# Where one layer's modulation steps are traced, how many go with a tile of the swiglus, and which queue loads them

## The chip, the cores and the metric

The kernel runs on one core of a Trainium2 chip. The time is device microseconds (us) of one execution; three executions of the kernel before gave 2858.24, 2849.52 and 2848.32 us, with a median of 2849.52 us. A fourth execution was profiled: it took 2853.62 us, and its span from the first instruction to the last is 2851.7 us.

## The reference

Two blocks run one after the other on a sequence of 512 tokens of width 1024, in float32. The first block has two layers: gated linear attention (GLA) and a swiglu, then latent attention (MLA) and a swiglu. The second block mixes a pooling and a convolution branch, and then gathers experts. Ahead of all this, each layer turns the conditioning vector `c` into six modulation vectors, and each of its two halves uses three of them:

```
c_act = silu(c)
for i in range(DEPTH):
    mod = c_act @ ada_w[i] + ada_b[i]
    sh1, sc1, g1, sh2, sc2, g2 = split(mod, 6)
    h = rmsnorm(x, norm_mix[i]) * (1 + sc1) + sh1
    x = x + g1 * mixer(h)
    h = rmsnorm(x, norm_ffn[i]) * (1 + sc2) + sh2
    x = x + g2 * swiglu(h)
```

`ada_w[i]` is 1024 x 6144, so a layer's modulation reads 24 MB; the second block has one such layer more.

## The kernel before, in words

Activations lie transposed: eight tiles `x[k]` of 128 channels x 512 tokens. Each projection is a sum of three matmuls, since the weights and the activations are split into a high and a low part (`whi`/`wlo`, `hh`/`hl`, `fh`/`fl`; line 241, ScalarE copies the high part and VectorE subtracts). Weights come as units of 1 MB (`raw<-wst`, line 268) from SyncE's queue, 16 blocks of 128 x 128 in each; two tiles of a swiglu's input projection, which make one tile of its hidden width, use one unit.

The modulation isn't computed on TensorE. `ada` (lines 315 to 325) is a Python generator. One step of it loads 128 rows of the transposed `ada_w` (512 KB, `araw`, of which there are two buffers, `ARAW`), issued by SyncE's queue (line 320), and multiplies and sums them against silu(c) on VectorE in one instruction (`dot`, line 313), called a dot below. Eight steps make one of the six vectors. A layer's `mods` columns 16:24 are its first gate, 24:32 and 32:40 the shift and the scale of its second norm, 40:48 its second gate.

`step(n)` (line 329) traces n further steps at the place in the code where it stands, and `rest()` all that are left. There are three such streams around the change:

- In the GLA, 24 steps of layer 0 (columns 16 to 40). The order of the GLA's parts is `GLA_ORDER` (line 58): q are projections of queries and keys, i the work inside chunks (`intra`: eight levels, at each of which GpSimd subtracts, ScalarE takes the exponential, VectorE multiplies twice in lines 637 and 638, TensorE multiplies in line 644 and VectorE copies under a mask in line 650), v values, r the output gate's projections, o the outputs. Three steps follow each q (line 708), two each r (line 717), and `rest()` stands ahead of the output projection (line 724). `gains` (line 339) makes the second norm's factor from the scale, before `output_norm` begins (line 727).
- In the first swiglu (`ffn(0)`), 56 steps: the last vector of layer 0 and all of layer 1 (line 760). `step(FST)`, with `FST` = 3, follows each of the 22 tiles of the hidden width (line 749), eleven in each half.
- In the second swiglu (`ffn(1)`), 48 steps of the second block's layer (line 945), with the same calls.

In each half of a swiglu eleven tiles are made (per tile: 48 matmuls, then silu on ScalarE, a product on VectorE in line 742, and the split into `fh` and `fl`), and then the output projection runs over them (lines 750 and 751). `output_norm` (line 451) runs the output projection of an attention in six full tiles, then the last two in halves together with the norm (`tail`, `modulated`).

The place in the code isn't the place in an engine's queue. The framework plans ahead with costs of its own and fixes each engine's order at build time: an instruction goes to its engine when its plan has it ready and the engine free; of several that are ready the one traced first goes first (weights are let ahead by `high_priority`). So a step may be planned far ahead of the place where it is traced, when its engine is free in the plan. On the chip the engines then run their instructions in that order, each waiting for its own inputs.

Of the kernel before, what the change touches and what calls it, by code (L numbers as in the profile page):

```python
# [21 lines left out]
P = 128  # L22
S = 512
D = 1024
KD = 8
# [29 lines left out]
FIRST = 3  # L55
M0 = 6
HNU = 4
GLA_ORDER = "q0 q1 i0 q2 i1 q3 i2 v0 r0 r1 i3 r2 r3 o0 o1 v1 r4 r5 r6 r7 o2 o3"
RECT = 64
KXL = 1  # L60
ST = (3, 2, 2)
ARAW = 2
APART = 4
FST = 3
SPILL = [NA // 2 + (2 * i + 1) * (P // 2 - NA // 2) // (2 * NSP) for i in range(NSP)]
LAST = 2
GSC = 2.0 ** 14
# [127 lines left out]
def block_kernel(ctx, tc, x_in, cs_in, wst, vec, cst, gmask, smask, pos, ada1, ada2, wgate, keys, ust, uex, vex, out):  # L195
    nc = tc.nc
    V, A_, T_, G_, SP = nc.vector, nc.scalar, nc.tensor, nc.gpsimd, nc.sync
# [10 lines left out]
    def bank(tag="mm"):  # L208
        return ps.tile([P, S], F32, tag=tag, bufs=4, name=tag)
# [14 lines left out]
    def vc(name, i, n=1):  # L224
        return vt[:, VOFF[name] + i:VOFF[name] + i + n]

    x = [keep.tile([P, S], F32, name=f"x{k}") for k in range(KD)]
    hh = [keep.tile([P, S], F32R, name=f"hh{k}") for k in range(KD)]
    hl = [keep.tile([P, S], F32R, name=f"hl{k}") for k in range(KD)]
    mods = [keep.tile([P, 48], F32, name=f"mod{l}") for l in range(3)]  # L230
# [27 lines left out]
    def blk(name, n=1, eng=None):  # L258
        while SEQ[state["i"]][0] == "pad":
            state["i"] += 1  # L260
        i = state["i"]
        assert SEQ[i][0] == name, (SEQ[i], name)
        u, o = divmod(i, UB)
        assert o + n <= UB
        if state.get("u") != u:
            with tc.high_priority(state["ahead"]):
                raw = wp.tile([P, UB * P], F32, tag="raw", bufs=RAW, name="raw")
                SP.dma_start(raw, wst[u])
                state["w"] = parts(raw, G_ if name in POOL_LO else eng)
            state["u"] = u  # L270
        state["i"] = i + n
        return part(state["w"], o * P, n * P)

    def mm3(out_, wh, wl, ah, al, first, last):
        T_.matmul(out_, wh, ah, start=first, stop=False)  # L275
        T_.matmul(out_, wh, al, start=False, stop=False)  # L276
        state["mm"] = T_.matmul(out_, wl, ah, start=False, stop=last)  # L277
# [15 lines left out]
    def proj(name, ah, al, tag="mm"):  # L293
        if state["pre"]:
            return state["pre"].pop(0)
        p = bank(tag)
        n = len(ah)
        for k in range(n):
            wh, wl = blk(name)
            mm3(p, wh, wl, ah[k], al[k], k == 0, k == n - 1)  # L300
        return p
# [9 lines left out]
    def dot(out_, w, sc, op=V.scalar_tensor_tensor):  # L311

        op(out=w, in0=w, scalar=1.0, in1=sc, op0=ALU.mult, op1=ALU.mult, accum_out=out_)  # L313

    def ada(l, w, sc, bias, pieces=range(6)):

        for p in pieces:
            for n in range(p * KD, (p + 1) * KD):
                raw = mn.tile([P, D], F32, tag="araw", bufs=ARAW, name="araw")
                SP.dma_start(raw, w[n * P:(n + 1) * P, :])  # L320
                dot(mods[l][:, n:n + 1], raw, sc)
                if n % KD == KD - 1:
                    m = mods[l][:, p * KD:(p + 1) * KD]
                    V.tensor_add(m, m, bias[:, p * KD:(p + 1) * KD])
                yield
# [3 lines left out]
    def step(n=1):  # L329
        for _ in range(n):  # L330
            next(side["g"], None)

    def rest():
        for _ in side["g"]:
            pass

    def gains(l, which, g):

        o = sca[:, (l * 2 + which) * KD:(l * 2 + which + 1) * KD]
        sc_ = mods[l][:, (1 + 3 * which) * KD:(2 + 3 * which) * KD]  # L340
        V.scalar_tensor_tensor(o, sc_, 1.0, g, op0=ALU.add, op1=ALU.mult)
        return o
# [90 lines left out]
    def tail(name, ah, al, gate, sqs, norm):  # L433

        ws = [[blk(name) for _ in ah] for _ in range(2)]
        for half in range(2):
            cs = halves(half)
            for i, w in enumerate(ws):
                n = KD - 2 + i
                p = bank()  # L440
                for k, (wh, wl) in enumerate(w):
                    mm3(p[:, cs], wh, wl, ah[k][:, cs], al[k][:, cs], k == 0, k == len(ah) - 1)
                residual(n, p, gate, cs)
                for sq, scale in sqs:
                    sq.add(x[n], scale=scale and scale(n), half=half)
            norm(half)

    def residual(n, p, gate, cs=slice(0, S)):
        V.scalar_tensor_tensor(x[n][:, cs], p[:, cs], gate[:, n:n + 1], x[n][:, cs], op0=ALU.mult, op1=ALU.add)

    def output_norm(name, ah, al, gate, gain, shift, first):

        sq = Sq(mn, "a", KD, D)
        for n in range(KD - 2):
            residual(n, proj(name, ah, al), gate)
            sq.add(x[n])
        tail(name, ah, al, gate, [(sq, None)],
             lambda half: modulated(bcast(sq.rsqrt("n", half)), gain, shift, half))
        ahead(first, hh, hl)
# [5 lines left out]
    with tc.tile_pool(name="st", bufs=1, reuse_waits="tile") as st, tc.high_priority(2 * AHEAD):  # L465
# [62 lines left out]
        w = weights()  # L528
# [9 lines left out]
        for k in range(KD):  # L538
# [11 lines left out]
            w = w_  # L550
# [4 lines left out]
    with tc.tile_pool(name="gla", bufs=1, reuse_waits="tile") as gp:  # L555
# [147 lines left out]
        bs, n = gates()  # L703
        for what in GLA_ORDER.split():
            kind, h = what[0], int(what[1])
            if kind == "q":
                qk[h] = [first.pop(0) if first else qk_tile(i) for i in range(2)]
                step(3)
            elif kind == "i":
                ins[h] = intra(bs[h], *qk[h])  # L710
            elif kind == "v":
                vn[h] = values()
            elif kind == "r":
                p = proj("gla_w_in", hh, hl)
                sr[h] = gp.tile([P, S], F32, tag="sr", bufs=4, name="sr")
                A_.activation(sr[h], p, AF.Silu)
                step(2)
            else:
                if h == 2:
                    for i, o in enumerate(og):  # L720
                        split(hh[i], hl[i], o)
                    og = []
                og += output(h, vn[h // 2], [sr[2 * h], sr[2 * h + 1]], *ins[h])
        rest()
        for i, o in enumerate(og):
            split(hh[4 + i], hl[4 + i], o)
        output_norm("gla_w_out", hh, hl, mods[0][:, 16:24], gains(0, 1, vc("norm_ffn", 0, KD)),
                    mods[0][:, 24:32], "ffn_w_in")


    def ffn(l, sqs, norm, first):
        gate = mods[l][:, 40:48]
        norm_ = state["norm"]
        with tc.tile_pool(name=f"ffn{l}", bufs=1, reuse_waits="tile") as fp:
            for half in range(2):
                fh, fl = [], []
                for i in range(11):
                    p = proj("ffn_w_in", hh, hl)
                    s = fp.tile([P, S], F32, tag="s", bufs=2, name="s")
                    A_.activation(s, p, AF.Silu)  # L740
                    p = proj("ffn_w_in", hh, hl)
                    V.tensor_mul(s, s, p)
                    a = fp.tile([P, S], F32R, name=f"fh{i}")
                    c = fp.tile([P, S], F32R, name=f"fl{i}")
                    split(a, c, s)
                    fh.append(a)
                    fl.append(c)
                    with tc.issue_after(norm_.ins):
                        step(FST)
                for n in range(KD - 2 * half):  # L750
                    residual(n, proj("ffn_w_out", fh, fl), gate)
                    if half:
                        for sq, scale in sqs:
                            sq.pool = sq.pool or fp
                            sq.add(x[n], scale=scale and scale(n))
            rest()
            tail("ffn_w_out", fh, fl, gate, sqs, norm)
            ahead(first, hh, hl)
# [52 lines left out]
    with tc.tile_pool(name="mla", bufs=1, reuse_waits="tile") as mp:  # L811
# [124 lines left out]
        for h in range(MLA_H):  # L936
# [2 lines left out]
            attend(h, prs.pop(h))  # L939
            if h + 2 < MLA_H:  # L940
                queries(h + 2)
        output_norm("mla_w_out", hh, hl, mods[1][:, 16:24], gains(1, 1, vc("norm_ffn", KD, KD)),
                    mods[1][:, 24:32], "ffn_w_in")

    side["g"] = ada(2, ada2, silu_c(1), vc("ada_b_2", 0, 48))


# [25 lines left out]
    with tc.tile_pool(name="b2", bufs=1, reuse_waits="tile") as bp:  # L973
# [45 lines left out]
        for g in range(4):  # L1019
            p = proj("w_in_2", hh, hl)  # L1020
            step(4)
            w = WINDOWS[g]
# [63 lines left out]
        for n in range(8):  # L1086
# [1 line left out]
            V.tensor_mul(sg[8 + n], sg[8 + n], p)  # L1088
            V.tensor_add(sg[n], sg[n], sg[8 + n])
            split(hh[n], hl[n], sg[n])  # L1090
        output_norm("w_out_2", hh, hl, mods[2][:, 16:24], gains(2, 1, vc("norm2_g_2", 0, KD)),
                    mods[2][:, 24:32], "w_query_2")

    main.close()
# [2 lines left out]
    with tc.tile_pool(name="peer", bufs=1, reuse_waits="tile") as pp:  # L1097
# [38 lines left out]
        with tc.tile_pool(name="sel", bufs=1, reuse_waits="tile") as sp:  # L1136
# [179 lines left out]
            for h in range(PH):  # L1316
                qq, ql = [], []
                for half in range(2):
# [3 lines left out]
                    l = sp.tile([P, P], F32, name=f"ql{h}_{half}")  # L1322
# [21 lines left out]
            for j2 in range(NA // 2):  # L1344
                up(j2, eng=V)
                if j2 == HNU:
                    mark = state["mm"]

        with tc.tile_pool(name="exp", bufs=1, reuse_waits="tile") as ep:
# [81 lines left out]
            for g in range(P // GJ):  # L1431
# [13 lines left out]
                for half in range(2):  # L1445
# [12 lines left out]
                    for dd in range(4):  # L1458
                        n = half * 4 + dd
# [95 lines left out]
```

## Time and profile before

| What | Value |
|---|---|
| median of three runs | 2849.52 us |
| the profiled execution | 2853.62 us, span 2851.7 us |
| TensorE busy | 95% of the span |
| VectorE busy | 75% |
| ScalarE, GpSimd busy | 37%, 29% |
| GLA after its first norm | about 66 to 282 us of the span |
| its output projection and norm | 282 to 336 us |
| first swiglu | 336 to about 720 us |
| second swiglu | 933 to about 1310 us |

Busy shares are averages over stages with different limits. What one engine's idle time costs is read from the stage: which wait ends last there.

### The profile page before, as it was taken

The page shows a single profiled execution, that of the slowest core. Times are in us where ns is not written, and L with a number is a line of the kernel's source. Part 1 is how long each engine was busy: PE and PEld are TensorE (multiplying, and loading weights), DVE is VectorE, ACT ScalarE, POOL GpSimd, SP SyncE. Part 2 cuts the span into 40 slices and gives each one's busy share as a digit, 9 for nine tenths or more (in the row PEclk, how much of TensorE's full clock was granted, in tenths as well). Part 3 has the DMA queues.
Part 4 walks back from the last instruction along what each step waited for, and adds up shares of the span by engine and source line. Part 5 has one row for each costly group of instructions (what it writes and reads, how often), then busy time and mean ns, then how long its engine had stood idle before and what let it go on. Part 6 is the DMA issues. An engine that isn't in the chain of part 4 may idle for free. (4 is left out here: it accounts for less than half of the span.)

```text
span 2851.7 us, 39033 instructions
## 1 busy us (share of the span) xinstructions
PE 2717.1 (95%) x14889; PEld 2447.4 (86%) x14889; DVE 2150.5 (75%) x3981; ACT 1064.6 (37%) x1530; POOL 816.3 (29%) x586
## 2 busy tenths in 40 slices
PE   6799999999999999999999999899999999999998
PEld 4677887888778878888778888889999999999998
DVE  8874766435776773348976798888899889988996
ACT  4443322222543322234443336654333343333332
POOL 4531100001011000001631423433545445545561
PEclk9899999999999999999999999999999999999999
DMA  6441477432212673222223236666999999999993
GB/s 265 140 136 60 145 260 258 140 104 78 74 45 74 229 257 129 94 89 90 74 89 103 77 110 192 204 191 229 362 350 342 356 339 346 336 341 329 345 342 136
DMA packets 184363, 560.62 MB, mean 197 GB/s; under 512 B 13248, under 2 KB 66912, under 8 KB 157680
## 3 DMA queue, kind: packets, MB, share of 16 engines
q1 hardware_dynamic: 142352, 407.08, 41.0%
q0 software_dynamic: 41472, 151.01, 14.2%
q8 instruction: 117, 1.92, 0.3%
q14 instruction: 70, 0.57, 0.1%
q10 hardware_dynamic: 352, 0.03, 0.0%
HBM read 527.32 MB, written 30.75 MB: 196 GB/s over the span
## 5 line engine op out<-in xcount | busy, mean ns | idle before, releaser
L241 ACT CAST whi<-raw 128x1024 fp32r<-128x1024 f32 x510 | 535.1, 1051 | 1197.4 <-PE mm L276 617.5
L277 PE MATMUL mm<-hh,wlo 128*128 128x512 f32 (+2 forms) x2544 | 899.4, 354 | 9.4 <-DVE wlo L241 9.4
L276 PE MATMUL mm<-hl,whi 128*128 128x512 f32 (+2 forms) x2544 | 900.6, 355 | 7.4 <-DVE hl L427 6.6
L275 PE MATMUL mm<-hh,whi 128*128 128x512 f32 (+2 forms) x2544 | 899.9, 355 | 2.0 <-ACT hh L426 1.4
L241 DVE TENSOR_TENSOR wlo<-raw,whi 128x1024 fp32r<-128x1024 f32 x472 | 585.7, 1242 | 264.8 <-ACT whi L241 251.5
L277 PEld LDWEIGHTS mm<-hh,wlo 128*128 128x128 f32 x2544 | 482.5, 190 | 59.3 <-DVE wlo L241 11.6
L276 PEld LDWEIGHTS mm<-hl,whi 128*128 128x128 f32 x2544 | 482.9, 190 | 56.0 <-DVE hl L427 7.9
L275 PEld LDWEIGHTS mm<-hh,whi 128*128 128x128 f32 x2544 | 482.6, 190 | 49.1 <-ACT hh L426 1.8
L241 POOL TENSOR_TENSOR wlo<-raw,whi 128x1024 fp32r<-128x1024 f32 x38 | 90.9, 2398 | 907.5 <-ACT whi L241 866.2
L1376 POOL DMA_INDIRECT rows<-vex,eidx x144 | 223.9, 1555 | 203.3 <-DVE y L1390 186.7
L1376 POOL DMA_INDIRECT rows<-uex,eidx x144 | 215.9, 1499 | 217.0 <-DVE rows L1380 162.6
L313 DVE SCALAR_TENSOR_TENSOR araw<-araw,sc 128x1024 f32<-128x1024 f32 x128 | 160.5, 1256 | 96.5 <-DMA araw<-ada 95.9
L1390 DVE SCALAR_TENSOR_TENSOR y<-rows,act,y 128x1024 f32<-128x1024 f32 x142 | 181.7, 1280 | 6.9 <-DMA rows<-vex,eidx 6.3
L1380 DVE SCALAR_TENSOR_TENSOR rows<-rows,hn 128x1024 f32<-128x1024 f32 x144 | 169.8, 1220 | 15.2 <-DMA rows<-uex,eidx 15.2
L275 PE MATMUL mm<-fh,whi 128*128 128x512 f32 (+1 forms) x396 | 148.0, 374 | 10.2 <-ACT fh L241 10.2
L276 PE MATMUL mm<-fl,whi 128*128 128x512 f32 (+1 forms) x396 | 148.3, 375 | 2.0 <-DVE fl L241 2.0
L277 PE MATMUL mm<-fh,wlo 128*128 128x512 f32 (+1 forms) x396 | 147.6, 373 | 0.0
L1306 PE MATMUL acc<-oa,ob 128*128 128x128 f16 x736 | 95.6, 297 | 18.6 <-POOL oa L1297 11.0
L1297 POOL TENSOR_TENSOR oa<-o,o 128x1024 f16<-128x1024 f16 x30 | 81.8, 2742 | 83.4 <-DVE o L1283 57.4
L1306 PEld LDWEIGHTS <-ob 128*128 128x128 f16 x736 | 81.5, 119 | 27.9 <-issue 18.9
L1309 ACT ACTIVATE stage<-acc 128x512 f32<-128x512 f32 x92 | 90.0, 1103 | 27.5 <-PE acc L1306 15.7
L275 PEld LDWEIGHTS mm<-fh,whi 128*128 128x128 f32 x396 | 77.1, 195 | 23.4 <-ACT fh L241 11.1
(1381 smaller groups left out, 4685.4 us busy)
## 6 DMA issues: line engine op xcount, KB each, us to landing
raw<-wst SPq DMA_DIRECT2D x127, 1024.0 KB, 4.9
araw<-ada SPq DMA_DIRECT2D x128, 512.0 KB, 4.5
raw<-ust SPq DMA_DIRECT2D x64, 1024.0 KB, 6.5
raw<-vex SPq DMA_DIRECT2D x64, 1024.0 KB, 7.8
gd<-stage SPq DMA_DIRECT2D x23, 1024.0 KB, 4.8
gt<-gd SPq DMA_DIRECT2D x16, 1472.0 KB, 10.3
aw<-ada SPq DMA_DIRECT2D x16, 512.0 KB, 9.4
spilled<-a SPq DMA_DIRECT2D x24, 184.0 KB, 3.4
```

The source lines that it names most:

```text
L241: state["split"] = (A_.copy(hi, src), (eng or V).tensor_sub(lo, src, hi.bitcast(F32)))
L275: T_.matmul(out_, wh, ah, start=first, stop=False)
L276: T_.matmul(out_, wh, al, start=False, stop=False)
L277: state["mm"] = T_.matmul(out_, wl, ah, start=False, stop=last)
L313: op(out=w, in0=w, scalar=1.0, in1=sc, op0=ALU.mult, op1=ALU.mult, accum_out=out_)
L1297: (G_ if i and (s * 4 + q0) // TQ % POOL_OA else V).tensor_mul(o.rearrange("p q (a b) t -> p q a b t", b=16), o8[i][:, qs, :, None, :].to_ ...
L1306: T_.matmul(p[:, t * P:(t + 1) * P], ob[:, q, :, t], oa[i][:, q, :, t], start=i == 0, stop=i == 1)
L1309: A_.mul(st[:, :, t1:t1 + 4].rearrange("p j t -> p t j"), p.rearrange("p (t j) -> p t j", t=4), 1.0 / GSC)
L1376: G_.indirect_dma_start(out=r, out_offset=None, in_=uex if up_ else vex, in_offset=bass.IndirectOffsetOnAxis(ap=eidx[:, n:n + 1] if n < P ...
L1380: V.scalar_tensor_tensor(r, r, 1.0, hn if n < P else hx, op0=ALU.mult, op1=ALU.mult, accum_out=act[:, n:n + 1])
L1390: V.scalar_tensor_tensor(z, r, act[:, n:n + 1], z, op0=ALU.mult, op1=ALU.add)
```

## The change

Five things are changed. The GLA's steps no longer follow the q parts, and follow only the six last r parts, two each; two more (`GST`) follow each of the six full tiles of `output_norm`, where `rest()` and the making of the norm's factor (`gain`, now a function that is called there) now stand. `FST` is 2, and one step follows each full tile of a swiglu's output projection. The loads of layer 1 and of the second block's layer (`l` of 1 and 2) are issued by GpSimd's queue; those of layer 0 still by SyncE's. In the two later calls of `output_norm` no stream is left, so that only the place of `gain` moves there.

```diff
+GST = 2
...
-FST = 3
+FST = 2
...
-                SP.dma_start(raw, w[n * P:(n + 1) * P, :])
+                (G_ if l else SP).dma_start(raw, w[n * P:(n + 1) * P, :])
...
         for n in range(KD - 2):
             residual(n, proj(name, ah, al), gate)
             sq.add(x[n])
+            step(GST)
+        rest()
+        gain = gain()
         tail(name, ah, al, gate, [(sq, None)],
...
                 qk[h] = [first.pop(0) if first else qk_tile(i) for i in range(2)]
-                step(3)
...
                 A_.activation(sr[h], p, AF.Silu)
-                step(2)
+                if h >= 2:
+                    step(2)
...
-        rest()
         for i, o in enumerate(og):
             split(hh[4 + i], hl[4 + i], o)
-        output_norm("gla_w_out", hh, hl, mods[0][:, 16:24], gains(0, 1, vc("norm_ffn", 0, KD)),
+        output_norm("gla_w_out", hh, hl, mods[0][:, 16:24], lambda: gains(0, 1, vc("norm_ffn", 0, KD)),
...
                 for n in range(KD - 2 * half):
                     residual(n, proj("ffn_w_out", fh, fl), gate)
+                    step()
```

## Rows read from the trace of the kernel before

**Rows 1.** The page, part 1: busy time of each engine, its share of the span, and its instructions.
```profile
PE 2717.1 (95%) x14889; PEld 2447.4 (86%) x14889; DVE 2150.5 (75%) x3981; ACT 1064.6 (37%) x1530; POOL 816.3 (29%) x586
```
**Rows 2.** Stretches of the span: from and to, length, busy time of PE, PEld, DVE, ACT and POOL with their instructions, the granted TensorE clock (1.00 is 2.4 GHz, 0.50 is 1.2 GHz), the DMA engines' share, GB/s.
```profile
66.00:97.00 31.00, 23.80 (x83) 16.95 (x81) 26.10 (x25) 20.64 (x34) 15.49 (x11) 0.86 0.43 152
97.00:165.00 68.00, 56.62 (x315) 48.62 (x316) 60.75 (x93) 25.11 (x40) 43.30 (x48) 0.91 0.40 140
...
200.00:282.00 82.00, 79.49 (x413) 64.97 (x412) 36.09 (x91) 27.90 (x44) 12.29 (x9) 1.00 0.15 52
...
336.00:447.00 111.00, 111.00 (x517) 92.86 (x515) 79.17 (x118) 32.93 (x43) 0.00 (x0) 1.00 0.75 256
447.00:460.00 13.00, 6.75 (x23) 4.90 (x22) 9.16 (x14) 2.01 (x3) 0.00 (x0) 0.74 0.82 284
...
1045.00:1058.00 13.00, 7.00 (x19) 5.02 (x18) 9.20 (x15) 1.57 (x2) 0.00 (x0) 0.74 0.69 247
```
**Rows 3.** TensorE's waits, longest first: whom it waited for, us in total, times, the longest. The first row is of the stretch 66 to 165 us, the second of 336 to 540, the third and fourth of 934 to 1085.
```profile
PE acc L644 <- DVE e L638: 16.2, 6, 7.4
...
PE mm L275 <- ACT fh L241: 6.0, 1, 6.0
...
PE mm L275 <- ACT fh L241: 4.3, 1, 4.3
PE mm L276 <- DVE fl L241: 1.7, 1, 1.7
```
**Rows 4.** VectorE's groups of instructions in 97 to 165 us of the GLA (busy us, mean ns of one, then the idle time before them).
```profile
L313 DVE SCALAR_TENSOR_TENSOR araw<-araw,sc 128x1024 f32<-128x1024 f32 x13 | 17.7, 1368 | 0.0
L650 DVE COPY_PREDICATED at<-gm,acc 128x512 f32<-128x512 uint8 x21 | 15.3, 729 | 3.7 <-ACT e L634 3.4 <-PE acc L644 0.3
L638 DVE TENSOR_TENSOR e<-e,k 128x256 f32<-128x256 f32 x21 | 13.8, 655 | 0.0
L637 DVE TENSOR_TENSOR e<-e,q 128x256 f32<-128x256 f32 x20 | 13.6, 679 | 1.8 <-ACT e L634 1.6
```
**Rows 5.** VectorE in order of time, just ahead of the first level of the first `intra` (start, us, instruction).
```profile
88.59 2.32 DVE L313 SCALAR_TENSOR_TENSOR araw<-araw,sc 128x1024 f32<-128x1024 f32 x1
...
94.14 2.28 DVE L313 SCALAR_TENSOR_TENSOR araw<-araw,sc 128x1024 f32<-128x1024 f32 x1
...
96.35 0.41 DVE L637 TENSOR_TENSOR e<-e,q 128x256 f32<-128x256 f32 x1
96.69 0.41 DVE L638 TENSOR_TENSOR e<-e,k 128x256 f32<-128x256 f32 x1
```
**Rows 6.** The end of the first half's input projection in the first swiglu, in order of time: three of VectorE's instructions, and TensorE's first matmul after its wait (in brackets the idle time before an instruction, and what ended it).
```profile
449.44 1.23 DVE L313 SCALAR_TENSOR_TENSOR araw<-araw,sc 128x1024 f32<-128x1024 f32 x1 [3.72 <-DMA araw<-ada]
450.66 1.23 DVE L313 SCALAR_TENSOR_TENSOR araw<-araw,sc 128x1024 f32<-128x1024 f32 x1
451.81 0.68 DVE L742 TENSOR_TENSOR s<-s,mm 128x512 f32<-128x512 f32 x1
...
453.20 0.80 PE L275 MATMUL mm<-fh,whi 128*128 128x512 f32 x1 [5.95 <-ACT fh L241]
```
**Rows 7.** VectorE in order of time over one tile of the same input projection, from one product of line 742 to the next, and SyncE's load that follows the dot at 352.74 (it is SyncE's row).
```profile
352.74 1.22 DVE L313 SCALAR_TENSOR_TENSOR araw<-araw,sc 128x1024 f32<-128x1024 f32 x1 [2.60 <-DMA araw<-ada]
...
354.00 0.33 SPq L320 DMA_DIRECT2D araw<-ada  x1
...
356.26 0.68 DVE L742 TENSOR_TENSOR s<-s,mm 128x512 f32<-128x512 f32 x1
357.63 1.23 DVE L313 SCALAR_TENSOR_TENSOR araw<-araw,sc 128x1024 f32<-128x1024 f32 x1 [0.69 <-DMA araw<-ada]
...
360.02 1.23 DVE L313 SCALAR_TENSOR_TENSOR araw<-araw,sc 128x1024 f32<-128x1024 f32 x1 [0.47 <-DMA araw<-ada]
...
365.05 1.23 DVE L313 SCALAR_TENSOR_TENSOR araw<-araw,sc 128x1024 f32<-128x1024 f32 x1 [2.66 <-DMA araw<-ada]
...
366.35 1.23 DVE L313 SCALAR_TENSOR_TENSOR araw<-araw,sc 128x1024 f32<-128x1024 f32 x1
...
368.63 0.68 DVE L742 TENSOR_TENSOR s<-s,mm 128x512 f32<-128x512 f32 x1
```
**Rows 8.** The same products of line 742 in the second half of the first swiglu, where no step is left.
```profile
606.68 0.69 DVE L742 TENSOR_TENSOR s<-s,mm 128x512 f32<-128x512 f32 x1 [3.38 <-PE mm L277]
...
617.56 0.69 DVE L742 TENSOR_TENSOR s<-s,mm 128x512 f32<-128x512 f32 x1 [3.37 <-PE mm L277]
```
**Rows 9.** The dots' group on VectorE in 336 to 447 us (busy us, mean ns | idle before, and what ended it), and, of the tile `araw` over the whole span, the time from SyncE's issue of its load to its landing.
```profile
L313 DVE SCALAR_TENSOR_TENSOR araw<-araw,sc 128x1024 f32<-128x1024 f32 x36 | 44.0, 1225 | 30.4 <-DMA araw<-ada 30.1
...
DMA to landing us min/median/max: 3.2/4.5/8.0
```
**Rows 10.** Line 1376, the experts' gather at the end of the kernel: GpSimd issues loads of 128 rows of 4 KB each, 512 KB as `araw` has (duration on GpSimd in ns, min/median/max), and the time from issue to landing.
```profile
L1376 POOL DMA_INDIRECT rows<-uex,eidx x144: 937/1681/4131, 1964.1 to 2368.2; - x144
L1376 POOL DMA_INDIRECT rows<-vex,eidx x144: 939/1235/5076, 2370.5 to 2796.3; - x144
...
DMA to landing us min/median/max: 4.1/7.3/12.4
```
**Rows 11.** VectorE's group that reads the rows of that gather, from the page, part 5.
```profile
L1380 DVE SCALAR_TENSOR_TENSOR rows<-rows,hn 128x1024 f32<-128x1024 f32 x144 | 169.8, 1220 | 15.2 <-DMA rows<-uex,eidx 15.2
```
**Rows 12.** The making of the second norm's factor in the GLA (duration in ns, min/median/max, first and last start).
```profile
L341 DVE SCALAR_TENSOR_TENSOR sca<-mod,vt x1: 168/168/168, 194.8 to 194.8; 128x8 f32<-128x8 f32 x1
```

More of the change, by code (lines that the diff above doesn't have):

```diff
@@ L941, in block_kernel @@
                 queries(h + 2)
-        output_norm("mla_w_out", hh, hl, mods[1][:, 16:24], gains(1, 1, vc("norm_ffn", KD, KD)),
+        output_norm("mla_w_out", hh, hl, mods[1][:, 16:24], lambda: gains(1, 1, vc("norm_ffn", KD, KD)),
                     mods[1][:, 24:32], "ffn_w_in")
@@ L1090, in block_kernel @@
             split(hh[n], hl[n], sg[n])
-        output_norm("w_out_2", hh, hl, mods[2][:, 16:24], gains(2, 1, vc("norm2_g_2", 0, KD)),
+        output_norm("w_out_2", hh, hl, mods[2][:, 16:24], lambda: gains(2, 1, vc("norm2_g_2", 0, KD)),
                     mods[2][:, 24:32], "w_query_2")
```

## The prediction

> **What bounds the kernel now.** I read the page first, then stretches of the span, then TensorE's waits in those stretches, and last VectorE's instructions in order of time around each wait. TensorE is busy for 95% of the span [rows 1], so an edit can win only where TensorE waits or runs at the lower clock. Of the places that the change touches three have such a loss.
>
> The first is the GLA from 66 to 165 us. VectorE is busy for 60.75 of the 68 us from 97 to 165, TensorE for 56.62 [rows 2]: VectorE is the bound there. TensorE's waits for the products of line 638 sum to 16.2 us, 7.4 of them at the first level [rows 3]. Just ahead of that level two dots stand, stretched to 2.32 and 2.28 us [rows 5], and from 97 to 165 us there are 13 more, 17.7 of VectorE's 60.75 us [rows 4]. The granted clock is 0.86 and 0.91 of 2.4 GHz [rows 2]. From 200 to 282 us VectorE is busy for only 36.09 of 82 us, and TensorE loses 2.5 us [rows 2].
>
> The other two are the ends of the first halves' input projections in the swiglus. TensorE is busy for all of 336 to 447 us, and then for 6.75 of 13 us at a clock of 0.74; at 1045 us it is 7.00 of 13 [rows 2]. That is 6.25 + 6.0 us of idle time. Some 2 us come on top of each, since half the stretch runs at 1.2 GHz after TensorE stood still: about 16 us in all. TensorE waits for the last tile's `fh` [rows 3]; its product stands on VectorE behind two dots, the first of which waited 3.72 us for its load [rows 6].
>
> Why VectorE is late there shows over one tile. From product to product it takes 368.63 - 356.26 = 12.4 us, with four dots between [rows 7]; TensorE's own tile takes 617.56 - 606.68 = 10.9 us [rows 8]. VectorE falls back by 1.5 us a tile, without an effect until the half ends. It isn't short of time: of 111 us it is busy for 79.17 [rows 2], and 30.1 us are waits for the loads [rows 9]. With two buffers two dots take one round: issue, landing, dot. Two rounds a tile make the 12.4 us. The number to note is four: the code traces three steps a tile, and 36 dots ran from 336 to 447 us [rows 9], about ten tiles. The planner pulls steps ahead of their place, as fast as it believes the two buffers turn round.
>
> **The change, part by part.** Steps later in the GLA. No instruction goes or comes: 24 loads and 24 dots stay, and the loads stay on SyncE. What changes is precedence. Before, six steps are traced ahead of the first `intra`, three more ahead of the second; now all 24 come behind the fourth. A dot can then enter the intra work only where the plan sees VectorE free. The later dots of this stretch were fillers already, so I take the early ones alone to move. (a) The dot at 94.14 no longer holds up the first level: -2.3 us, of a wait of 7.4. The one at 88.59 stands in the gates' work, which is traced ahead of all steps in either kernel; it may stay. (b) Of the 13 dots from 97 to 165 us I let four go, 4 x 1.37 = 5.5 us of VectorE. TensorE, which is idle for 11.4 of those 68 us, gets about half: -2.7. Bounds: 0 if they stay fillers, -11.4 and some 6 us of clock if all 13 go. (c) Less waiting should spare a stretch of low clock: -1. (d) The dots come later, among the outputs' chains. VectorE has 46 free us there, but loads there may be late for their dots, as in the swiglus, and a state update waits behind them: +1, between 0 and 5 x 1.2 = +6. Sum: -5 us.
>
> Twelve steps in `output_norm`, and the later factor. By the same planning their dots should be over before 282 us. If they are not, 12 dots are six rounds of 6.2 us, 37 us, beside six tiles of some 5.5 us (half a swiglu tile's 48 matmuls), 33 us: +4 us and a late norm. The factor's instruction is 0.168 us, once per call [rows 12], and moves to where VectorE has room: 0.
>
> Two steps a tile and one in the output projection. The plan already ran four a tile where three were traced. Lowering the number traced doesn't slow a stream that isn't held by it: 0, with -16 us as the bound if two a tile were really kept.
>
> Loads on GpSimd's queue. 96 issues of 0.33 us leave SyncE and 96 go to GpSimd, about 1 us each by the shortest gather issues [rows 10]. GpSimd has no instruction from 336 to 447 us [rows 2], so nothing stands behind them. SyncE's queue didn't hold the loads up either: the dot at 352.74 ends at 353.96, the next load is issued at 354.00 [rows 7]. So what counts is the landing. SyncE's takes 3.2 us at best and 4.5 in the middle [rows 9]. Of GpSimd's the trace has only the gather, 4.1 at best, and 7.3 in the middle beside a nearly full DMA [rows 10]. Bounds for the change: -1 us a load (it no longer stands behind a 1 MB weight unit in one queue) and +2.8 (7.3 - 4.5). At 0.75 DMA share I stay near the best values: +0.9 for the round without a weight unit beside it, -0.8 for the one with, so 0.1 us a tile. I take 0 for both swiglus, with 8 us to either side. If the cover, VectorE's lag without effect, is used up, each further us goes to the end-of-half wait.
>
> One rule speaks against this part. Rows first: the dots of the gather, the same form, take 1220 ns beside GpSimd's issues [rows 11], against 1225 in the swiglu [rows 9]; the issues take 0.94 us at least and 1.24 or 1.68 in the middle [rows 10]. The Trainium skill, "SBUF — State Buffer", section "SBUF: two separate sides", warns that GpSimd can't write descriptors while VectorE holds the port pair that both share, so that such a load starves where SyncE's would not. It names VectorE's 2-port modes; whether dots with two inputs do it no run here shows. By the rule the issues would sit at the longer values, 0.74 us later a round, 1.5 us a tile; by the shortest rows, 0. The slower rival below takes up that case.
>
> Sum: -5 + 0 = -5 us. Against the profiled execution that is 2848.6 us. It ran 4.1 us above the median, so the forecast for the median is 2844.5 us.
>
> **The rivals.** Two a tile is kept (faster). The plan's rate follows the traced one, two dots a tile need one round of 6.2 us, VectorE keeps up, and both end-of-half waits go: -5 - 16 = -21, 2828 us. For it: the remedy is exactly there. Against: four ran where three were traced.
>
> The intra work is rid of its dots (faster). All 13 leave; TensorE gets most of 11.4 us and of the clock's 0.09 x 68 = 6 us, and the first level's 2.3: -18, 2832 us. Against it: fillers stay fillers.
>
> Loads land later (slower). VectorE's order holds four dots a tile whatever the landing is. If GpSimd's loads land 0.9 us later (4.1 - 3.2), two rounds cost 1.8 us a tile more. The first swiglu has some 8 such tiles before its half ends (eight of its steps still load from SyncE), the second 10: 18 x 1.8 = +32, less 5: +27, 2876 us. It decides from 0.14 us a load on (18 x 2 x 0.14 = 5). For it: every gather row is longer than SyncE's shortest. Against: beside a weight unit a queue of its own helps.
>
> The order hardly moves. The plan fills with dots what it filled before, and loads are alike: 2849 us.
>
> **How the numbers follow.** Forecast 0.48, two a tile 0.18, intra rid of dots 0.10, later landing 0.16, no move 0.08. A run can tell 0.5% (14 us) from no change. Faster takes the two faster rivals nearly whole and the lower edge of the forecast: 0.28. Slower is the later landing with little beside it: 0.16. The rest, 0.56, is within. The forecast's own range is 2834 to 2857. The range for 8 in 10 reaches to the faster rivals, 2823, and over most of the later landing, 2869, which leaves out about 0.1 on each side.
>
> **What would show it.** Right: the dot ahead of the first level gone and TensorE's wait there near 5 us; 9 or 10 dots from 97 to 165 us; four dots still between products in the swiglus, `araw` landing at 4.5 to 5 us from GpSimd, and an idle stretch of about 6 us at the ends of both first halves. Wrong: two or three dots a tile and no such wait (faster), or landings over 5.3 us and waits over 10 us there (slower); or steps left over at the GLA's output norm, with TensorE waiting for the factor.

## The result and the profile after

The changed kernel took 2873.09 us (median of four runs, 2868.75 to 2873.91), the kernel before 2850.74 us beside it. The two medians are 22 us apart; the ratio of the runs is 1.0057, with a 95% interval of 1.0041 to 1.0074, which is 16 us. By both the kernel got slower. The forecast was 2844.5 us, a gain of 5, and the range ended at 2869. The sign was missed. The median lies 4 us beyond the range; by the ratio the time would be 2867 us, just inside it.

The profiled execution after has a span of 2870.6 us. Part 1 of its page, which answers to [rows 1]:

```profile
PE 2717.1 (95%) x14889; PEld 2445.2 (85%) x14889; DVE 2154.1 (75%) x3981; ACT 1066.8 (37%) x1530; POOL 853.3 (30%) x682
```

TensorE's busy time is the same to 0.1 us, so the 18.9 us by which this span is longer are idle time of TensorE. The stretches show where it lies. Columns as in [rows 2]:

```profile
66.00:97.00 31.00, 23.44 (x87) 17.16 (x85) 26.69 (x25) 22.74 (x38) 18.27 (x15) 0.83 0.35 126
97.00:165.00 68.00, 57.11 (x317) 48.41 (x317) 62.45 (x96) 24.90 (x39) 43.33 (x47) 0.92 0.39 128
200.00:282.00 82.00, 79.45 (x417) 65.39 (x418) 36.48 (x91) 28.51 (x44) 12.30 (x9) 1.00 0.16 57
336.00:447.00 111.00, 109.76 (x514) 91.35 (x513) 74.77 (x112) 30.40 (x40) 14.55 (x27) 1.00 0.71 242
447.00:460.00 13.00, 4.53 (x19) 2.90 (x17) 7.73 (x11) 3.00 (x4) 2.12 (x4) 0.81 0.68 244
460.00:473.00 13.00, 9.58 (x30) 7.38 (x31) 9.74 (x16) 2.62 (x3) 2.65 (x5) 0.66 0.71 243
```

The GLA's rows hardly differ from [rows 2]. The end of the first half's input projection does: TensorE was idle for 6.25 us there and now is for 8.47 from 447 to 460 and 3.42 from 460 to 473. A clock of 0.81 and 0.66 over 13 us each is 4.9 + 8.8 = 13.7 us at 1.2 GHz, where before had 0.74, or 6.8 us. Much of that passed while TensorE stood still. The stretch at the lower clock, cut where TensorE's work begins again, first in the trace after and then in that of before:

```profile
455.10:463.10 8.00, 0.00 (x0) 0.00 (x0) 4.74 (x7) 0.64 (x2) 1.59 (x3) 0.50 0.59 206
463.10:468.80 5.70, 5.38 (x12) 3.91 (x13) 4.12 (x8) 0.93 (x1) 0.82 (x2) 0.51 0.97 344
...
450.10:453.20 3.10, 0.00 (x1) 0.00 (x1) 3.10 (x6) 0.67 (x2) 0.00 (x0) 0.50 0.47 129
453.20:456.90 3.70, 3.41 (x7) 2.42 (x8) 2.78 (x5) 0.89 (x1) 0.00 (x0) 0.50 0.99 353
```

TensorE worked at 1.2 GHz for 5.7 us after and for 3.7 us before. At half the clock that costs half of each, 2.9 and 1.9 us, so the clock adds about 1 us to the longer wait. TensorE's waits, in the stretches 66 to 165, 336 to 540 and 934 to 1105 us, beside [rows 3]:

```profile
PE acc L648 <- DVE e L642: 18.2, 10, 7.6
...
PE mm L276 <- ACT fh L242: 10.6, 1, 10.6
PE mm L278 <- DVE wlo L242: 2.2, 3, 1.0
...
PE mm L276 <- ACT fh L242: 10.8, 1, 10.8
```

The wait for the last tile's `fh` grew from 6.0 to 10.6 us in the first swiglu and from 4.3 (with 1.7 for `fl`) to 10.8 in the second. Three waits for `wlo`, the low part of a weight that VectorE makes, are new in the first; they sum to 2.2 us. VectorE in order of time just ahead of the first, and TensorE's first matmul after it, as in [rows 6]:

```profile
453.73 1.22 DVE L314 SCALAR_TENSOR_TENSOR araw<-araw,sc 128x1024 f32<-128x1024 f32 x1 [0.87 <-DMA araw<-ada]
...
459.36 1.23 DVE L314 SCALAR_TENSOR_TENSOR araw<-araw,sc 128x1024 f32<-128x1024 f32 x1 [3.26 <-DMA araw<-ada]
...
460.59 1.23 DVE L314 SCALAR_TENSOR_TENSOR araw<-araw,sc 128x1024 f32<-128x1024 f32 x1
...
461.74 0.68 DVE L745 TENSOR_TENSOR s<-s,mm 128x512 f32<-128x512 f32 x1
...
463.13 0.80 PE L276 MATMUL mm<-fh,whi 128*128 128x512 f32 x1 [10.62 <-ACT fh L242]
```

The picture is that of before, some 10 us later: the last product stands behind two dots, and they behind their loads. Are the loads slower, then? The tile `araw` in the trace after, beside [rows 9] (issues on GpSimd with their duration in ns, min/median/max, then issue to landing in us), and VectorE's dots in 97 to 165 and in 336 to 447 us:

```profile
L321 POOL DMA_DIRECT2D araw<-ada x96: 527/530/752, 357.2 to 1096.2; - x96
...
DMA to landing us min/median/max: 3.4/4.6/8.2
```

```profile
L314 DVE SCALAR_TENSOR_TENSOR araw<-araw,sc 128x1024 f32<-128x1024 f32 x13 | 18.0, 1402 | 0.0
...
L314 DVE SCALAR_TENSOR_TENSOR araw<-araw,sc 128x1024 f32<-128x1024 f32 x34 | 41.4, 1224 | 35.0 <-DMA araw<-ada 35.0
```

They land as before, 4.6 us in the middle against 4.5. The 4.6 are of all 128 loads, 32 of them SyncE's; of the 96 from GpSimd alone it is 4.65, and of the same 96 before, from SyncE, 4.60. But fewer dots ran in those 111 us (34 for 36), with more waiting (35.0 us for 30.4). What comes between a dot and the next load of its buffer shows in one pair of rows:

```profile
366.78 1.22 DVE L314 SCALAR_TENSOR_TENSOR araw<-araw,sc 128x1024 f32<-128x1024 f32 x1
...
368.30 0.53 POOL L321 DMA_DIRECT2D araw<-ada  x1 [1.75 <-DVE araw L314]
```

The dot ends at 368.00 and GpSimd, which has nothing else to do, begins the issue at 368.30. Over all 96 such pairs of the trace the mean is 0.30 us and the longest 0.33. On SyncE it is 0.04 [rows 7], which is also the middle of its pairs in the trace of before.

To see in which stage the time went I took, for each profiled execution, how much longer than in the profile of before a stage is (us, by the starts of the residuals that end the stages; negative is shorter):

| Kernel | to the end of the GLA's norm | first swiglu | MLA | second swiglu | the rest | sum |
|---|---|---|---|---|---|---|
| after | +1.7 | +9.3 | +4.0 | +5.0 | -1.1 | +18.9 |
| queue_only | -2.4 | +6.0 | +4.4 | +7.6 | +3.2 | +18.8 |
| queue_again | -0.1 | +9.4 | +4.6 | +6.5 | +5.0 | +25.4 |
| steps_only | -1.3 | +0.5 | +4.5 | -0.2 | +5.4 | +8.9 |
| sp_count | -0.1 | +6.2 | -0.6 | +2.6 | -1.8 | +6.3 |
| capped_dots | -2.7 | +7.5 | +3.6 | +7.1 | +2.0 | +17.5 |
| held_before | -1.3 | -8.2 | +4.3 | -9.1 | +3.9 | -10.4 |
| held_pool | -0.4 | -8.2 | +3.7 | -9.1 | +0.7 | -13.3 |
| held_sp | 0.0 | -8.3 | +1.2 | -8.5 | +3.7 | -11.9 |
| gla_held | -4.4 | -8.1 | +2.1 | -8.5 | -0.1 | -19.0 |

Each is one execution. `queue_only` and `queue_again` are the same kernel, so a stage is known to some 3 us. The rest holds of the change only the place where one factor is made; it scatters from -1.8 to +5.4. Of the first swiglu's 9.3 us in the kernel after, the longer wait for `fh` is 4.6, the waits for `wlo` 2.2 and the clock about 1.

The MLA is 4 us longer in most profiles, with SyncE's loads as with GpSimd's. There the longer time goes with the granted clock. From 740 to 931 us, first before and then in `steps_only`, both with SyncE's loads:

```profile
740.00:931.00 191.00, 182.89 (x1009) 150.41 (x1008) 133.87 (x327) 76.99 (x153) 21.70 (x12) 1.00 0.17 57
...
740.00:931.00 191.00, 183.71 (x979) 150.10 (x978) 130.41 (x318) 74.57 (x148) 21.70 (x12) 0.97 0.17 57
```

It is 1.00 before and in `sp_count`, 0.99 in `held_sp` and `gla_held`, 0.98 in the kernel after, `capped_dots` and `held_pool`, and 0.97 in the four others. The MLA's column follows this order, and 0.03 of 191 us is 5.7 us. Why the clock falls there in some profiles and not in others stays open.

### The profile page after: what moved, and what is told of

The parts are those of the page before. It is cut to its first block, busy times and chain, and to the rows that moved or that the text cites. A ratio compares the mean times of both kernels' runs of the same rounds, so it can differ in the third digit from the quotient of the medians.

```text
span 2870.6 us, 39035 instructions
## 1 busy us (share of the span) xinstructions
PE 2717.1 (95%) x14889; PEld 2445.2 (85%) x14889; DVE 2154.1 (75%) x3981; ACT 1066.8 (37%) x1530; POOL 853.3 (30%) x682
## 4 chain that ended last, share of the span: by engine, by line
PE 64%; DVE 16%; issue 10%; POOL 4%; DMA 4%; ACT 2%; POOLq 0%; SPq 0%; DVEq 0%; ACTq 0%
PE mm L277 14%; PE mm L276 14%; PE mm L278 14%; PE acc L278 5%; PE acc L277 5%; PE acc L276 5%; DVE wlo L242 2%; DMA araw<-ada 2%; DVE yc L1007 1%; DVE oa L1301 1%; PE acc L1310 1%; POOL araw L321 1%; DMA raw<-vex 1%; PE acc L648 1%; PE acc L364 1%
## 5 line engine op out<-in xcount | busy, mean ns | idle before, releaser
L1380 POOL DMA_INDIRECT rows<-vex,eidx x144 | 212.1, 1473 | 217.4 <-DVE y L1394 200.6
L321 POOL DMA_DIRECT2D araw<-ada x96 | 51.2, 533 | 306.8 <-DVE araw L314 285.3
```

Source lines behind the costliest of these rows:

```text
L321: (G_ if l else SP).dma_start(raw, w[n * P:(n + 1) * P, :])
L1380: G_.indirect_dma_start(out=r, out_offset=None, in_=uex if up_ else vex, in_offset=bass.IndirectOffsetOnAxis(ap=eidx[:, n:n + 1] if n < P ...
```

## The experiments

**Which part costs: the queue or the steps?** `queue_only` is the kernel before with one line changed. `steps_only` is the changed kernel without that line.

```diff
-                SP.dma_start(raw, w[n * P:(n + 1) * P, :])
+                (G_ if l else SP).dma_start(raw, w[n * P:(n + 1) * P, :])
```

> The kernel before with one line changed: the loads of layer 1 and of the second block go to GpSimd's queue. Theory (the queue makes the swiglus later: each freed buffer is taken up 0.27 us later by GpSimd than by SyncE, and the plan puts one and two dots more ahead of the last product of the two first halves): the end-of-half waits are about 10.8 and 11 us as in the changed kernel, not 6.1 and 4.4, and the time is 2862 to 2872 us. Rival (the steps' new places in the attention and the swiglus make the loss): waits as before, 2848 to 2854 us.

> The changed kernel with all loads back on SyncE. Theory: waits of about 6 and 4.4 us at the ends of the first halves as before, the time 2847 to 2855 us, since the dots' order in the swiglus does not depend on the number of steps traced a tile. Rival: 2862 us or more.

Measured: `queue_only` 2874.6 us, ratio 1.0069 (1.0045 to 1.0094); `steps_only` 2855.98 us, ratio 1.0007 (0.9995 to 1.0018). TensorE's waits in the swiglus, first of `queue_only`, then of `steps_only`:

```profile
PE mm L275 <- ACT fh L241: 9.9, 1, 9.9
...
PE mm L275 <- ACT fh L241: 10.4, 1, 10.4
```

```profile
PE mm L276 <- ACT fh L242: 5.7, 1, 5.7
...
PE mm L276 <- ACT fh L242: 4.3, 1, 4.3
PE mm L277 <- DVE fl L242: 1.7, 1, 1.7
```

Both times lie 1 to 3 us above what was expected, 2862 to 2872 and 2847 to 2855; the kernel before beside them took 2855.43 us, 5 more than in the first comparison. By the ratios the one line is the whole loss. Everything else in the change, three steps or two a tile, the steps after the output projection's tiles and the GLA's later steps, leaves both waits where they were and the time within 0.2%.

**What if the steps really follow their tiles?** `held_pool` is the changed kernel with each swiglu step ordered behind the split that closes its tile (`fl`, line 242); `held_sp` is the same with SyncE's loads; `held_before` is the kernel before with nothing but this hold, three steps a tile.

```diff
-                    with tc.issue_after(norm_.ins):
+                    with tc.issue_after(norm_.ins), tc.issue_after(state["split"][1].ins):
                         step(FST)
```

> The changed kernel, with the dots of a swiglu tile's steps also held behind that tile's last subtraction on VectorE, so that two a tile are two in the order too. Theory (the wait at the end of a half is what the dots ahead of the last product have gathered): both waits gone, 16 us off the kernel before, 2830 to 2840 us, though the loads come from GpSimd. Rival (loads from GpSimd cost by themselves, in landing or in contention with the weights): 2850 us or more, with TensorE waiting for weights or products elsewhere.

> The same held order with all loads on SyncE. Theory: within 3 us of the held kernel with GpSimd's loads, since a later landing costs nothing while no dot stands ahead of a product that TensorE waits for: 2830 to 2840 us. Rival (the queue matters by itself): 8 us or more faster than with GpSimd's loads.

> The kernel before, with nothing changed but the hold: a swiglu tile's three steps have their dots behind that tile's last subtraction. Theory: about three dots a tile, 9.3 us of rounds in a tile of 10.9, so VectorE keeps up and both waits go: 2836 to 2846 us. Rival (two a tile is needed): a wait of 2 us or more stays at the end of a first half.

Measured: `held_pool` 2840.5 us, ratio 0.9954 (0.9937 to 0.9971); `held_sp` 2842.31 us, 0.9960 (0.9945 to 0.9974); `held_before` 2836.97 us, 0.9936 (0.9910 to 0.9961). The first two lie 0.5 and 2.3 us above the expected 2840, and `held_before` within its range. Two stretches of `held_pool`, over the ends of the first halves, and one tile of it on VectorE:

```profile
336.00:460.00 124.00, 124.00 (x572) 103.73 (x571) 74.77 (x104) 37.22 (x47) 10.29 (x19) 1.00 0.58 205
934.00:1060.00 126.00, 126.00 (x566) 104.66 (x565) 75.28 (x107) 35.50 (x44) 14.34 (x27) 1.00 0.59 209
```

```profile
374.84 0.69 DVE L745 TENSOR_TENSOR s<-s,mm 128x512 f32<-128x512 f32 x1 [3.38 <-PE mm L278]
...
377.38 1.22 DVE L314 SCALAR_TENSOR_TENSOR araw<-araw,sc 128x1024 f32<-128x1024 f32 x1
...
378.52 1.22 DVE L314 SCALAR_TENSOR_TENSOR araw<-araw,sc 128x1024 f32<-128x1024 f32 x1
...
385.72 0.69 DVE L745 TENSOR_TENSOR s<-s,mm 128x512 f32<-128x512 f32 x1 [3.38 <-PE mm L278]
```

TensorE never stops, at full clock. Two dots stand in a tile, neither waits for its load, and the product waits for TensorE and not the reverse; from product to product it is 10.9 us, TensorE's own tile. VectorE no longer falls back, and then the queue doesn't matter: GpSimd's 0.9954 and SyncE's 0.9960 are the same within their intervals. Nor does the number traced: in `held_before` three steps follow each tile, and its stretches are as full:

```profile
336.00:460.00 124.00, 124.00 (x569) 103.58 (x568) 82.72 (x120) 36.49 (x45) 0.00 (x0) 1.00 0.70 241
934.00:1060.00 126.00, 126.00 (x564) 104.62 (x563) 82.45 (x120) 35.45 (x44) 0.00 (x0) 1.00 0.70 239
```

**By which step does the queue cost?** In the traces of the kernel after and of `queue_only` the last product of the first half has 63 dots ahead of it in the first swiglu and 119 in the second; before and `steps_only` have 62 and 117. The plan, made at build time with its own costs, put more dots there once the queue was another. `capped_dots` is `queue_only` with the 63rd and 118th dot and those that follow held behind that product.

```diff
-                    V.tensor_mul(s, s, p)
+                    prod = V.tensor_mul(s, s, p)
+                    if half == 0:
+                        prod_ = prod
...
-                        step(FST)
+                        for _ in range(FST):
+                            with ExitStack() as held:
+                                if half and i * FST + _ >= (5, 4)[l]:
+                                    held.enter_context(tc.issue_after(prod_.ins))
+                                step()
```

> The kernel before with the loads of the later layers on GpSimd's queue, and the dots from the 63rd (first swiglu) and the 118th (second) on held behind the last product of the first half, so that as many dots stand ahead of that product as in the kernel before (62 and 117, not 63 and 119). Theory (each dot ahead of the product costs half a round, 3.1 us, and the later take-up 0.54 us a tile): the waits fall from 10.3 and 10.8 us to about 7 and 5 us, the time to 2862 to 2868 us beside 2874 with the queue alone. Rival (the whole loss is the later take-up): waits within 1.5 us of those with the queue alone.

Measured: 2871.07 us, ratio 1.0050 (1.0034 to 1.0065), 3 us above the expected range. 62 and 117 dots ran ahead of the product, as they should. TensorE's waits in the two swiglus:

```profile
PE mm L275 <- ACT fh L241: 10.3, 1, 10.3
PE mm L276 <- DVE fl L241: 1.4, 1, 1.4
...
PE mm L275 <- ACT fh L241: 5.7, 1, 5.7
PE mm L276 <- DVE fl L241: 3.3, 1, 3.3
```

In the second swiglu the wait for `fh` is 5 us shorter than in `queue_only`, as expected, but the wait for `fl` took 3.0 of them back. In the first nothing was won where 3 us were expected. The held dots had gone between the product and `fl`, which TensorE needs next. So this kernel doesn't separate count from queue, and the count had to be tried from the other side.

`sp_count` is the kernel before with SyncE's loads and the count that GpSimd's loads had brought: four steps are traced a tile, and the last product of the first half is ordered behind the 63rd and the 119th dot (`done` lists the dots). Its trace has 63 and 119 dots ahead of that product. Ahead of the other products the order isn't quite that of GpSimd's loads: in the second swiglu five dots stand between the last two products, where GpSimd's order has four there and one more further ahead. `queue_again` is `queue_only` once more, beside it.

```diff
-FST = 3
+FST = 4
...
-                    V.tensor_mul(s, s, p)
+                    with ExitStack() as held:
+                        if half == 0 and i == 10:
+                            held.enter_context(tc.issue_after(done[(62, 118)[l]].ins))
+                        V.tensor_mul(s, s, p)
```

> The kernel before with its loads on SyncE, four steps traced a tile, and the product of the first half's last tile ordered behind the 63rd and the 119th dot: the plan then has the dots between the products as it has them with the loads on GpSimd (63 and 119 ahead of the last product, where before has 62 and 117). Theory of the count: GpSimd's queue costs by the dots that it lets the plan put ahead of the last product, and each of them is half a round, 3.1 us. Then the waits of TensorE at the ends of the first halves grow from 7.4 and 6.9 us to about 10.5 and 13, and the time is 9 us above before (5 to 13). Rival, the take-up: the same order costs little as long as SyncE issues the loads, since a freed buffer is taken up 0.3 us sooner; the waits stay within 3 us of before's and the time within 4 us of it. Control: the plan's count is met, and the dots run 62 to 64 and 118 to 120 ahead of the last product.

> The kernel queue_only once more, beside the one with the same order of dots on SyncE's queue. Theory of the count: the two take the same time within 4 us, and their waits at the ends of the first halves agree within 2 us. Rival, the take-up: this one is 8 us or more above the other. By either its time is 2866 to 2880 us, as in its first run, and its waits there near 11.4 and 11.9 us; that they differ by more than 2 us from these would say that a single profile doesn't resolve them.

Measured: `sp_count` 2861.1 us, ratio 1.0030 (1.0019 to 1.0042), +8.6 us; `queue_again` 2876.73 us, ratio 1.0079 (1.0059 to 1.0098), +22.5 us. The waits of `sp_count`, then those of `queue_again`:

```profile
PE mm L275 <- ACT fh L241: 10.0, 1, 10.0
PE mm L276 <- DVE fl L241: 1.0, 1, 1.0
...
PE mm L275 <- ACT fh L241: 8.5, 1, 8.5
PE mm L276 <- DVE fl L241: 0.6, 1, 0.6
```

```profile
PE mm L275 <- ACT fh L241: 11.0, 1, 11.0
...
PE mm L275 <- ACT fh L241: 11.1, 1, 11.1
```

Neither theory holds alone. The count on SyncE's queue cost in all what was expected of it, 8.6 us of 9, but not swiglu by swiglu. One dot more came with waits 4.7 us longer (11.0 for 6.3), and two dots more with 3.1 (9.1 for 6.0), where 3.1 and 6.2 were counted; only the sum bears the theory out. And the same count with GpSimd's loads cost 14 us more, where the theory of the count allowed 4. The two intervals don't overlap. By the table above the two swiglus of `sp_count` are 8.8 us longer than before's, and those of the three profiles with GpSimd's loads in this order 13.6 to 15.9. So of about 15 us in the swiglus some 9 are dots that the plan put further ahead, and some 6 the queue itself, each as uncertain as the stages of single profiles are.

The size of the second part shows in the time from the first product to the last of a first half, over the dots between them. With SyncE's loads (before, `steps_only`, `sp_count`, two swiglus each) it is 111.6 to 116.5 us for 35 to 37 dots, 3.12 to 3.19 a dot; with GpSimd's (after, `queue_only`, `queue_again`, `capped_dots`) 116.4 to 121.2 us for 35 to 37, 3.15 to 3.34, in the mean 3.25 against 3.15; the two ranges overlap. A freed buffer is taken up 0.30 - 0.04 = 0.26 us later. With two buffers in turn half of that falls on each dot: 0.13 us, an estimate, where 0.10 was measured. Over 74 dots of both first halves 0.10 us is 7 us, near the 6.

That the take-up is the cause of this second part rests on this agreement and on the equal landings: of the loads for these dots alone, issue to landing is 4.81 us in the mean with SyncE and 4.82 with GpSimd. It is argued and not shown, since no kernel here changes the take-up alone. The ratios are 14 us apart and the swiglus 5 to 7; 5 more lie in the MLA of the profiles, where `queue_again` has its clock at 0.91 from 760 to 800 us and `sp_count` 1.00, and the remainder in the scatter of the rest. `steps_only` has the same longer MLA at the same lower clock with SyncE's loads, so I don't put it down to the queue.

**Would a real move of the GLA's steps pay?** `gla_held` is `held_pool` with the GLA's steps ordered behind the last masked copy of the fourth `intra`.

```diff
-                    step(2)
+                    with tc.issue_after(state["at"].ins):
+                        step(2)
```

> The held kernel with GpSimd's loads, and in the attention all 24 dots held behind the last masked copy of the fourth intra work. Theory that dots bound that stretch: TensorE's waits from 97 to 165 us shrink by half or more and the time falls by 8 to 18 us below the held kernel's 2840, if the norm's factor isn't late. Rival (the dots only fill; the chain from GpSimd over ScalarE to VectorE is the bound there): within 5 us of 2840.

Measured: 2834.61 us, ratio 0.9926 (0.9902 to 0.9951), the lowest median of all, though its interval overlaps those of the other held kernels. From 97 to 165 us it reads as follows, with TensorE's waits there, first in `gla_held` and then in `held_pool`:

```profile
97.00:165.00 68.00, 61.37 (x364) 52.28 (x364) 43.64 (x70) 28.63 (x43) 33.09 (x46) 1.00 0.15 50
```

```profile
PE acc L648 <- DVE e L642: 6.5, 7, 1.3
...
PE acc L648 <- DVE e L642: 12.4, 8, 2.2
```

No dot is left there, and the waits are about half, as by the theory that dots bound that stretch. VectorE is busy for 17 us less, TensorE for 4.75 us more than before, and the clock is 1.00 for 0.91. The last masked copy starts at 177.3 us, 16.7 sooner than the 194.0 of before. But at the first residual of the output projection only 3.5 are left, and the median is 6 us below that of `held_pool`, where the theory had 8 to 18 and its rival at most 5. From 200 to 282 us its dots stand as follows on VectorE, and the longest of TensorE's waits there is one for a state update behind them:

```profile
L314 DVE SCALAR_TENSOR_TENSOR araw<-araw,sc 128x1024 f32<-128x1024 f32 x16 | 21.4, 1347 | 10.2 <-DMA araw<-ada 10.2
```

```profile
PE acc L665 <- DVE st L675: 3.1, 1, 3.1
```

From 200 to 282 us TensorE is busy for 76.30 us where before has 79.49, and its clock is 0.96 for 1.00: 3.2 and 3.3 us, about half of the 13 that were lost again. That these are the work of the 16 dots fits the wait shown; for the other half no wait here stands. Against `held_pool` the profile is 4 us shorter up to the end of the norm; the ratios, 0.9926 and 0.9954, don't resolve more.

## Why the prediction was wrong

**The step that failed** is "I take 0 for both swiglus", with 8 us to either side, for the loads on GpSimd's queue. In the profile after the two swiglus are 9.3 + 5.0 = 14.3 us longer. The landing part was right: 4.65 us in the middle from GpSimd, inside the named 4.5 to 5. Two terms were missing; the runs show the second with its cost, and the first with its size but not alone.

- The round was put together of "issue, landing, dot". The time from the dot's end to the next issue was read on SyncE as 0.04 us [rows 7] and carried over to GpSimd, where the free engine was taken to react as fast. It took 0.30. That this is small hid that it recurs on each of 74 dots with no slack: VectorE's order was already behind TensorE, so each tenth arrives at the wait. Its share is the 6 us or so that the count leaves over.
- "Lowering the number traced doesn't slow a stream that isn't held by it" was right, but I kept the plan's order fixed under a change of queue too ("VectorE's order holds four dots a tile whatever the landing is"). The plan put one dot and two dots more ahead of the last products. At 3.15 us a dot these are 9.5 us, and `sp_count` measured 8.6 in sum.

**The slower rival** had the right sign, the right place and a fair point from which it decides: 0.14 us a load, where the queue added 0.26. Its mechanism was another (0.9 us of landing), and its 2876 is nearer the result by an overestimate of one term and the lack of another. "Over 10 us there" came, "landings over 5.3 us" didn't. The rule from the Trainium skill, "SBUF — State Buffer", section "SBUF: two separate sides", shows no sign of having acted. The issues beside dots kept to 0.53 us in the middle and 0.75 at most, the dots took 1224 ns, landings stayed, and the take-up is 0.30 to 0.33 us on every one of the 96 loads. Another page of the Trainium skill, "DMA: Bandwidth & Descriptors", section "Specifications", has about 1 us to the first byte from GpSimd and about 0.6 from SyncE. Half of that difference on each of 74 dots would be 15 us, an estimate by these figures of the Trainium skill. In these traces the landing counted from the issue shows no such difference, and the time ahead of the issue shows 0.26 us.

**Four a tile though two are traced** was right. `steps_only` has two traced and the same dots ahead of the products and the same waits as before. The rival "two a tile is kept" fell for the reason named, and its price was good: -16 us for both waits, where `held_pool` has -17.3 in the two swiglus.

**The GLA** was forecast at -5 us and brought nothing: -1.3 us in `steps_only` and +1.7 after, in one and the same order of work.

- (a) The two dots ahead of the first level did go, and the first masked copy starts at 98.56 us in the trace after, where it was 102.30. TensorE's longest wait still is 7.6 us, not the 5 named; it only ends sooner. In `gla_held`, with no dot in the intra work at all, it is 9.2 us, so its length isn't the dots' doing; its end moves, from 97.25 us to 93.89 after and 92.40 there.
- (b) "Four of 13 go" failed: 13 dots still run from 97 to 165 us, at 1402 ns. The early start was lost there, and the last masked copy stands at 195.3 us for 194.0. Of my bounds the lower was the case, "0 if they stay fillers": steps traced later filled the same gaps, as in the swiglu.
- (c) No stretch of low clock was spared: 0.83 and 0.92 from 66 to 97 and from 97 to 165 us, where before had 0.86 and 0.91.
- (d) was undersized, as far as `gla_held` shows: once all 13 go, some 13 of 16.7 us are given back later, where I had +6 at most. The rival "rid of its dots" had -18 at the intra work, where 16.7 came, and no price for what came behind.

The twelve steps in `output_norm` and the later factor cost nothing that shows, as forecast: the stage to the end of the norm is between -2.7 and +1.7 us in all kernels but `gla_held`, with the change or without.

## What to carry to other kernels

Where an engine already lags and works through a fixed order, a load's full round counts, from the freed buffer to the issue as well as from the issue to the landing; a tenth of a microsecond each time can add up at the next wait (argued here, and not tried alone). A change of queue also changes what a planner believes, so read the new order and not only the new durations. The cure was an edge in the order and no number: holding each filler behind the work of its tile took 11 to 18 us off with either queue and with two or three steps a tile.

## What the hardware showed that I had not expected

- GpSimd with nothing else to run began a load 0.30 us after its buffer was free (0.33 at most), SyncE after 0.04 in the row shown; the issue itself took 0.53 us for 0.33.
- A plain 512 KB load from GpSimd landed as SyncE's did, 4.65 us in the middle for 4.60 (3.4/4.6/8.2 us over all loads after for 3.2/4.5/8.0 before), though the experts' gather of the same size had 4.1/7.3/12.4 and issues of 0.94 us at least [rows 10], where these issues took 0.53: the gather said little of it.
- The wait at the end of a half cost more than itself: in both traces the clock fell to 1.2 GHz within it and was still there when TensorE began to work again. But the longer wait cost little more of it: 5.7 us of work at the lower clock after 10.6 idle us, and 3.7 after 6.0.
